# A causal decoder trunk on one core: the activation and weight buffers placed at chosen remainders of a KB

## The chip, the cores and the metric

The kernel runs on one core of one Trainium2 chip. The core has a matrix engine (TensorE, PE in the profile; PEld is its weight load), a vector engine (VectorE, DVE), a scalar engine (ScalarE, ACT), GpSimd (POOL) and a queue that issues DMAs (SyncE, SP). On-chip memory (SBUF) has 128 partitions, and a tile takes the same bytes in each of them; matmuls write to a separate memory, PSUM. The metric is the device time of one execution in microseconds, as a median of several.

## The reference

A trunk of two layers over 256 positions with 2048 features, in float32. Each layer: a norm, an attention mixer and a residual; a norm, a gated MLP with a causal convolution of width 3 and a residual; then a gated per-layer input and a residual.

```python
for i in range(DEPTH):                       # DEPTH = 2
    a = rmsnorm(h, attn_norm[i])
    h = h + (sb_dilated_mixer if i % 2 == 0 else fox_mixer)(a, ...)
    h = h + conv_ffn(rmsnorm(h, ffn_norm[i]), w_up[i], conv_w[i], conv_b[i], w_down[i])
    gate = jax.nn.sigmoid(rmsnorm(h, ple_norm[i]) @ w_ple_gate[i])
    h = h + gate * (p[i] @ w_ple[i])
return rmsnorm(h, final_norm)
```

Layer 0 mixes with 8 stick-breaking and 8 dilated heads, layer 1 with 16 heads that have forget gates. The feed-forward width is 5632. Nearly all the arithmetic is in the products with the weights: w_in, w_out, w_up, w_down and w_ple_gate, some 450 MB that are read once.

## The kernel before

Features lie on partitions and positions along the free axis. A float32 product is made of three products in a rounded format (float32r): each operand is split into a rounded part and the rest, and `PARTS` lists the three pairs that are summed (rest times rest is left out). An activation buffer `act0` or `act1` has the shape [128, 16, 2, 256]: 16 k tiles, and for each the rounded part and the rest, 256 positions of 4 bytes, so each such row is 1 KB. `pact` is a small one of the same kind for the per-layer input.

The weights come as a stream of *units* in the order of their use (`UNITS`). A unit is mostly 4 k tiles by 256 columns. `issue_group` brings one or two of them with one DMA of up to 1 MB into one of three raw buffers `wr` (L149). `split_unit` makes the two parts of a unit in a weight buffer `w`: ACT casts the rounded part (L165), DVE subtracts it from the raw value (L166). Of `w` there are four buffers of 8 KB, taken in rotation from a pool, each with rows of 1 KB (256 columns of a part of a k tile). `unit` keeps three split units ahead of the one in use.

`gemm_unit` (L203) runs the 24 matmuls of a unit: for each half j of the columns, each k tile and each of the three pairs, one matmul with 128 columns of `w` as the stationary operand and one row of `act` (256 positions) as the moving one. `gemm_v` (L237) has the roles the other way: a 128-position half row of `act` is stationary, 256 columns of `w` move. One block of layer 1, `gemm_vf` (L250), has 272 columns, since the forget gates' 16 columns are joined to the values', and its rows in `w` are 1088 bytes long.

The order of the work is written out by hand. Per pair of heads come q, k and v (psq, psk, psv); the attention's small float32 matmuls (scs, sps, avp) are deferred by some units (`defer`, `tick`) and so fall between the units of the next products. Then come w_out (pso), per group of 256 feed-forward features w_up (psu) twice, per block of 7 or 8 groups w_down (psd), and w_ple_gate (psg, in the last step pse). In layer 0, q, k, v, up and gate read act0, and out and down read act1; in layer 1 the two are swapped. The small per-layer product (psp) reads pact.

SBUF is handed out pool by pool, in the order in which the pools are opened, and within a pool in the order of the tiles: `cpool` with h (16 KB), act0, act1 (32 KB each), pact (4 KB), pl (16 KB) and small constants, then `wpool` with the three `wr` and four `w`, then `work` with the scratch tiles. `t2_tile` gives out scratch tiles of 2 KB from seven (for the feed-forward's yg and yv, the norm's squares and rows, the gates).

Of the kernel before, what the change touches and what calls it, by code (L numbers as in the profile page):

```python
# [10 lines left out]
F32 = mybir.dt.float32  # L11
F32R = mybir.dt.float32r
# [5 lines left out]
P = 128  # L18
D = 2048
S = 256  # L20
# [5 lines left out]
KT = D // P  # L26
# [78 lines left out]
def trunk(ctx: ExitStack, tc: tile.TileContext, xT, pT, pos, gains, conv, bf, cst, wst, out):  # L105
    nc = tc.nc

    cpool = ctx.enter_context(tc.tile_pool(name="cpool", bufs=1))
    wpool = ctx.enter_context(tc.tile_pool(name="wpool", bufs=1))
    work = ctx.enter_context(tc.tile_pool(name="work", bufs=1))  # L110
    psum = ctx.enter_context(tc.tile_pool(name="psum", bufs=1, space=bass.MemoryType.PSUM))

    h = cpool.tile([P, KT, S], F32, name="h")
    bufs = [cpool.tile([P, KT, 2, S], F32R, name=f"act{i}") for i in range(2)]
    pact = cpool.tile([P, 2, 2, S], F32R, name="pact")
    pl = cpool.tile([P, KT, S], F32, name="pl")
    gn = cpool.tile([P, 7, KT], F32, name="gn")
    cv = cpool.tile([P, DEPTH, 2 * FT, 4], F32, name="cv")
# [13 lines left out]
        return psum.tile([P, 2, 512], F32, name=name, tag="at", bufs=2)  # L132

    def t2_tile(name, shape=(P, 2, S), dt=F32):
        return work.tile(list(shape), dt, name=name, tag="t2", bufs=7)

    def t3_tile(name, shape=(P, 768), dt=F32):
        return work.tile(list(shape), dt, name=name, tag="t3", bufs=4)
# [3 lines left out]
    at = {"group": 0, "off": 0, "unit": 0, "tick": 0, "rows": 0}  # L142

    def issue_group():
        g = GROUPS[at["group"]]
        n = sum(u[3] * u[5] for u in g)
        raw = wpool.tile([P, 2048], F32, name="wr", tag="wr", bufs=3)
        src = wst[at["off"]:at["off"] + P * n].rearrange("(p f) -> p f", p=P)
        nc.sync.dma_start(out=raw[:, :n], in_=src)  # L149
        at["off"] += P * n  # L150
        at["group"] += 1
        o = 0
        for u in g:
            m = u[3] * u[5]
            raws.append((u, raw[:, o:o + m].rearrange("p (k c) -> p k c", c=u[5])))
            o += m

    def split_unit():
        if not raws:
            issue_group()  # L160
        u, raw = raws.pop(0)
        kc, cw = u[3], u[5]
        w = wpool.tile([P, 2048], F32R, name="w", tag="w", bufs=4)
        w = w[:, :2 * kc * cw].rearrange("p (k s c) -> p k s c", s=2, c=cw)
        nc.scalar.copy(out=w[:, :, 0, :], in_=raw)  # L165
        nc.vector.tensor_sub(out=w[:, :, 1, :], in0=raw, in1=w[:, :, 0, :].bitcast(F32))  # L166
        at["unit"] += 1
        ready.append((u, w))
# [3 lines left out]
    def unit(kind, l, k0, c0):  # L172
        while len(ready) < LOOK and at["unit"] < len(UNITS):
            split_unit()
        u, w = ready.pop(0)
        assert (u[0], u[1], u[2], u[4]) == (kind, l, k0, c0), (u, kind, l, k0, c0)
        return u[3], w
# [97 lines left out]
    def norm_squares(op):  # L275
        hs = h[:, 2 * op:2 * op + 2, :]
        if op == 0:
            nc.scalar.activation(out=acc, in_=hs, func=AF.Square)
        else:
            sq = t2_tile("sq")  # L280
            nc.scalar.activation(out=sq, in_=hs, func=AF.Square)
            nc.vector.tensor_add(out=acc, in0=acc, in1=sq)
# [26 lines left out]
    def norm_rows(mixer):  # L309

        dg = t2_tile("nd", (P, 2, P))
        ps = at_tile("rps")
        for t in range(2):
            nc.vector.tensor_scalar_mul(out=dg[:, t, :], in0=ident, scalar1=rT[:, t:t + 1])
            if mixer is None:
                nc.tensor.matmul(ps[:, 0, t * P:(t + 1) * P], lhsT=ones, rhs=dg[:, t, :],
                                 start=t == 0, stop=True, skip_group_check=True)
        if mixer is None:
            return ps[:, 0, :S]
        dh, dl = t2_tile("ndh", (P, 2, P), F32R), t2_tile("ndl", (P, 2, P), F32R)  # L320
        nc.scalar.copy(out=dh, in_=dg)
        nc.vector.tensor_sub(out=dl, in0=dg, in1=dh.bitcast(F32))
        for i, x in enumerate((dh, dl)):
            nc.tensor.matmul(ps[:, 0, :S], lhsT=trir[:, 0, :], rhs=x, start=i == 0, stop=i == 1)
        nc.vector.tensor_copy(out=rb, in_=ps[:, 0, :S])
        if mixer:
            nc.vector.tensor_scalar_mul(out=rq, in0=rb, scalar1=SCALE)
# [309 lines left out]
    for l in range(DEPTH):  # L637
        st = {}
        if l == 0:
            split_unit()  # L640
            rest_of_start()
            for op in range(8):
                ple_up(0, op)
            for i in range(8):
                norm_parts(i, 0, X)
            constants()

            def squares():
                for i in range(8):
                    norm_squares(i)  # L650

            defer(2, squares)
            norm_finish(True)
# [164 lines left out]
```

## Time and profile before

| | |
|---|---|
| Median of 3 runs | 2437.55 us (2437.21 to 2438.25) |
| The profiled execution | 2438.14 us |
| Its span, first to last instruction | 2436.3 us |
| Granted TensorE clock | 0.997 |
| Instructions | 48002 |
| HBM read | 452.86 MB, 187 GB/s over the span |

The profile is that of one execution. A line of the groups has the source line, the engine, the operation, what it writes and reads, how often, then the busy time and the mean of one in ns, then the idle time of the engine before it with what ended it. TensorE's matmuls overlap, so the mean of one (276 ns) is longer than the distance from one to the next. That distance is read from the chain in order of time, where a piece has its start, its length (both in us) and the number of its instructions.

### The profile page before, as it was taken

How to read it: one execution, taken by the hardware profiler on the slowest of the kernel's cores; microseconds unless marked ns; L12 is line 12 of the kernel's file. 1: busy time of each engine (PE TensorE's matmuls, PEld its weight loads, DVE VectorE, ACT ScalarE, POOL GpSimd, SP SyncE). 2: the span in 40 equal slices, each digit the busy share in tenths (PEclk: the TensorE clock that was granted, in tenths of full speed). 3: DMA queues.
4: the chain of work that ended last, by engine and by line, in shares of the span. 5: the costliest groups of instructions: out<-in, count | busy, mean ns of one | idle time of the engine just before them, and what ended most of it. 6: DMA issues, size and time to landing. Idle time of an engine off the chain costs nothing.

```text
span 2436.3 us, 48002 instructions
## 1 busy us (share of the span) xinstructions
PE 2414.1 (99%) x20990; PEld 2400.5 (99%) x20990; DVE 1595.7 (65%) x2157; ACT 1228.3 (50%) x1548; POOL 2.5 (0%) x8
## 2 busy tenths in 40 slices
PE   8999999999999999999999999999999999999997
PEld 8999999999999999999999999999999999999997
DVE  7557666776567657767765555677765776567676
ACT  6554455555355445555554444555543554455553
POOL 0000000000000000000000000000000000000000
PEclk9999999999999999999999999999999999999998
DMA  7444445555555555555554444555555555555553
GB/s 268 169 177 173 169 177 191 194 197 198 190 191 192 188 208 190 191 185 203 187 184 170 165 169 165 190 191 192 195 198 194 191 192 189 203 195 186 189 198 120
DMA packets 66483, 458.06 MB, mean 188 GB/s; under 512 B 7408, under 2 KB 7424, under 8 KB 16608
## 3 DMA queue, kind: packets, MB, share of 16 engines
q1 hardware_dynamic: 66096, 454.53, 52.8%
q8 instruction: 164, 2.69, 0.4%
q0 software_dynamic: 176, 0.46, 0.1%
q14 instruction: 47, 0.39, 0.0%
HBM read 452.86 MB, written 2.10 MB: 187 GB/s over the span
## 4 chain that ended last, share of the span: by engine, by line
PE 97%; DVE 1%; DMA 1%; ACT 1%; issue 0%; SPq 0%; DVEq 0%; ACTq 0%
PE psu L203 39%; PE psd L203 20%; PE pso L203 7%; PE psk L203 7%; PE psv L237 7%; PE psq L203 7%; PE psg L203 7%; DMA wr<-in_w 1%; PE avp L520 1%; PE psp L203 0%; PE pse L716 0%; PE scs L469 0%; PE psv L250 0%; PE sps L511 0%; PE avp L522 0%; PE scs L467 0%
## 5 line engine op out<-in xcount | busy, mean ns | idle before, releaser
L166 DVE TENSOR_TENSOR w<-wr,w 128x1024 fp32r<-128x1024 f32 (+2 forms) x882 | 1051.4, 1193 | 701.2 <-ACT w L165 695.5
L165 ACT CAST w<-wr 128x1024 fp32r<-128x1024 f32 (+2 forms) x882 | 905.6, 1028 | 1082.5 <-PE psu L203 355.1
L203 PE MATMUL psu<-act,w 128*128 128x256 f32 x8448 | 959.3, 276 | 0.0
L203 PEld LDWEIGHTS psu<-act,w 128*128 128x128 f32 x8448 | 958.3, 188 | 0.0
L203 PE MATMUL psd<-act,w 128*128 128x256 f32 x4224 | 479.7, 276 | 0.0
L203 PEld LDWEIGHTS psd<-act,w 128*128 128x128 f32 x4224 | 479.2, 188 | 0.0
L203 PE MATMUL psq<-act,w 128*128 128x256 f32 x1536 | 185.2, 279 | 1.2 <-DVE w L166 1.0
L203 PEld LDWEIGHTS psq<-act,w 128*128 128x128 f32 x1536 | 179.8, 188 | 2.1 <-DVE w L166 1.5
L203 PE MATMUL psk<-act,w 128*128 128x256 f32 x1536 | 180.0, 277 | 0.0
L203 PEld LDWEIGHTS psk<-act,w 128*128 128x128 f32 x1536 | 176.7, 188 | 0.0
L203 PE MATMUL pso<-act,w 128*128 128x256 f32 x1536 | 175.8, 277 | 0.0
L203 PEld LDWEIGHTS pso<-act,w 128*128 128x128 f32 x1536 | 174.9, 188 | 0.0
L237 PE MATMUL psv<-w,act 128*128 128x256 f32 x1440 | 172.7, 279 | 0.0
L237 PEld LDWEIGHTS psv<-w,act 128*128 128x128 f32 x1440 | 168.4, 188 | 1.1
L203 PE MATMUL psg<-act,w 128*128 128x256 f32 x1440 | 164.4, 276 | 0.0
L203 PEld LDWEIGHTS psg<-act,w 128*128 128x128 f32 x1440 | 163.7, 188 | 0.0
L616 DVE TENSOR_TENSOR u<-psu,rb 128x512 f32<-128x512 f32 x88 | 60.8, 691 | 33.3 <-PE psu L203 33.2
L622 DVE SCALAR_TENSOR_TENSOR yg<-u,cv,yg 128x256 f32<-128x256 f32 x176 | 73.3, 477 | 0.0
L622 DVE SCALAR_TENSOR_TENSOR yv<-u,cv,yv 128x256 f32<-128x256 f32 x176 | 73.3, 477 | 0.0
L619 ACT ACTIVATE yg<-u,cv 128x256 f32<-128x256 f32 x88 | 48.0, 594 | 1.0 <-DVE u L616 1.0
L619 ACT ACTIVATE yv<-u,cv 128x256 f32<-128x256 f32 x88 | 48.0, 593 | 0.0
L261 ACT CAST act<-yg 128x512 fp32r<-128x512 f32 x44 | 27.3, 621 | 39.1 <-DVE yg L632 39.1
(173 smaller groups left out, 886.5 us busy)
## 6 DMA issues: line engine op xcount, KB each, us to landing
wr<-in_w SPq DMA_DIRECT2D x388, 1024.0 KB, 4.8
wr<-in_w SPq DMA_DIRECT2D x36, 768.0 KB, 4.3
wr<-in_w SPq DMA_DIRECT2D x8, 896.0 KB, 4.6
wr<-in_w SPq DMA_DIRECT2D x7, 512.0 KB, 6.9
h<-in_x SPq DMA_DIRECT2D x4, 512.0 KB, 7.1
out_dram<-h SPq DMA_DIRECT2D x8, 256.0 KB, 2.4
wr<-in_w SPq DMA_DIRECT2D x2, 816.0 KB, 4.6
ct<-in_c SPq DMA_DIRECT2D x1, 841.0 KB, 6.6
```

The costliest lines, as they stand in the source:

```text
L165: nc.scalar.copy(out=w[:, :, 0, :], in_=raw)
L166: nc.vector.tensor_sub(out=w[:, :, 1, :], in0=raw, in1=w[:, :, 0, :].bitcast(F32))
L203: nc.tensor.matmul(ps[:, j, :], lhsT=w[:, k, s, js], rhs=act[:, k0 - koff + k, t, :], start=first and j + k + n == 0, stop=last and k == k ...
L237: nc.tensor.matmul(ps[:, t], lhsT=act[:, 4 * i + k, a, tsl], rhs=w[:, k, b], start=i + t + k + n == 0, stop=i == 3 and k == kc - 1 and n = ...
L261: nc.scalar.copy(out=dst[:, :, 0, :], in_=src)
L520: nc.tensor.matmul(av[:, 0, j * S:(j + 1) * S], lhsT=v[:, 0, js], rhs=w[:, j * S:(j + 1) * S], start=j == 0, stop=False, skip_group_check= ...
L616: nc.vector.tensor_mul(out=u[:, :, 2:], in0=ps, in1=rb2)
L619: nc.scalar.activation(out=y[:, j, :], in_=u[:, j, 2:], func=AF.Identity, bias=cv[:, l, t, 3:4], scale=cv[:, l, t, 2:3])
L622: nc.vector.scalar_tensor_tensor(out=y[:, j, :], in0=u[:, j, tap:tap + S], scalar=cv[:, l, t, tap:tap + 1], in1=y[:, j, :], op0=ALU.mult, ...
```

## The change

The activation and weight buffers move to the front of SBUF, into a pool of their own (`apool`). A helper `place` counts the bytes given out, from 16512 on, and puts an unused tile (gap) ahead of a buffer so that it starts at a chosen remainder of 1024: act0 at 0, act1 at 96, pact at 96, and the four weight buffers at 160, 256, 416 and 544. The weight buffers are four tiles with names, taken by the unit's number modulo 4, in place of four buffers of the pool `wpool`, which keeps the raw buffers and is opened ahead of `cpool`. The gaps take 1440 bytes. `t2_tile` has six tiles in place of seven. No instruction is added or removed.

```diff
+    apool = ctx.enter_context(tc.tile_pool(name="apool", bufs=1))
+    wpool = ctx.enter_context(tc.tile_pool(name="wpool", bufs=1))
     cpool = ctx.enter_context(tc.tile_pool(name="cpool", bufs=1))
-    wpool = ctx.enter_context(tc.tile_pool(name="wpool", bufs=1))
...
+    at_byte = [16512]
+
+    def place(shape, dt, name, rest):
+        n = (rest - at_byte[0]) % 1024
+        if n:
+            apool.tile([P, n // 4], F32, name=f"gap{at_byte[0]}")
+        t = apool.tile(shape, dt, name=name)
+        at_byte[0] += n + 4 * int(np.prod(shape[1:]))
+        return t
+
+    bufs = [place([P, KT, 2, S], F32R, f"act{i}", (0, 96)[i]) for i in range(2)]
+    pact = place([P, 2, 2, S], F32R, "pact", 96)
+    wbufs = [place([P, 2048], F32R, f"w{i}", (160, 256, 416, 544)[i]) for i in range(4)]
     h = cpool.tile([P, KT, S], F32, name="h")
-    bufs = [cpool.tile([P, KT, 2, S], F32R, name=f"act{i}") for i in range(2)]
-    pact = cpool.tile([P, 2, 2, S], F32R, name="pact")
...
-        return work.tile(list(shape), dt, name=name, tag="t2", bufs=7)
+        return work.tile(list(shape), dt, name=name, tag="t2", bufs=6)
...
-        w = wpool.tile([P, 2048], F32R, name="w", tag="w", bufs=4)
+        w = wbufs[at["unit"] % 4]
```

## The prediction

> **What bounds the kernel now.** I read the page first: the busy line, then the chain that ended last.
>
> ```profile
> PE 2414.1 (99%) x20990; PEld 2400.5 (99%) x20990; DVE 1595.7 (65%) x2157; ACT 1228.3 (50%) x1548; POOL 2.5 (0%) x8
> ...
> PE 97%; DVE 1%; DMA 1%; ACT 1%; issue 0%; SPq 0%; DVEq 0%; ACTq 0%
> PE psu L203 39%; PE psd L203 20%; PE pso L203 7%; PE psk L203 7%; PE psv L237 7%; PE psq L203 7%; PE psg L203 7%; DMA wr<-in_w 1%; PE avp L520 1%; PE psp L203 0%; PE pse L716 0%; PE scs L469 0%; PE psv L250 0%; PE sps L511 0%; PE avp L522 0%; PE scs L467 0%
> ```
>
> TensorE is never out of work: 97% of the chain is matmuls, and DVE (65%) and ACT (50%) have room. Who waits for whom says the same. ACT sits idle until matmuls free a weight buffer, while the longest wait of TensorE is 6.1 us in all, at the start.
>
> ```profile
> ACT w L165 <- PE psu L203: 355.1, 268, 2.1
> ...
> PE psp L203 <- ACT w L165: 6.1, 3, 5.6
> ```
>
> So the time is the number of matmuls times the distance from one start to the next, which I call the cadence. The chain in order of time gives it: a piece with its start, its length and its count. (In the groups of the page, busy over count says nearly the same: 959.3 us over 8448 is 113.6 ns.)
>
> ```profile
> 667.75 152.32 PE psu L203 x1344
> ...
> 2104.23 152.32 PE psu L203 x1344
> ```
>
> Both stretches, the first on act0 in layer 0 and the second on act1 in layer 1, have 152.32/1344 = 113.33 ns. The same lines show a second cadence.
>
> ```profile
> 231.28 8.16 PE psv L237 x72
> 239.44 0.22 PE scs L467 x2
> 239.66 0.43 PE scs L469 x2
> ...
> 240.75 2.83 PE psv L237 x24
> 243.58 8.48 PE psq L203 x72
> 252.06 0.65 PE sps L511 x6
> ```
>
> The matmuls of psv run at 8.16/72 = 113.33 ns, then a few fp32 matmuls of the attention come between, and the next ones run at 2.83/24 = 117.9 and 8.48/72 = 117.78 ns, on the same buffers, until the next interruption. So the cadence has two resting values, 113.33 and 117.78, and which one holds depends on when a run of matmuls starts. The third observation is the odd block of layer 1, 272 columns wide.
>
> ```profile
> 1212.64 6.73 PE psv L250 x54
> ```
>
> 6.73/54 = 124.6 ns. By its columns it should take 113.33 x 272/256 = 120.4 ns. What sets it apart is that its weight rows are 1088 bytes long, so the moving operand starts at another remainder of a KB, 64 bytes on, from one k tile to the next. This is the only stretch of the trace in which the remainder varies, and it is 4.2 ns per matmul slower than its width explains. I take from it that where an operand starts within a KB may matter to the cadence.
>
> **What the change does to that.** The remainders follow from the code. The new counter starts at byte 16512, which is 128 past a KB. Before, h lies there (16 KB), then act0, act1 and pact, all whole KBs: remainder 128 for all. The small constants behind them, each rounded up to 32 bytes, add 19,520 bytes (64 past a KB), so all seven weight buffers of 8 KB start at remainder 192. After, act0 is at 0, act1 and pact at 96, the weight buffers at 160, 256, 416 and 544.
>
> A matmul reads one operand from act and one from w. In the trace, the weight operand starts 64 or 576 bytes past the activations' remainder (L203, two column halves), or with the roles swapped (L237) 64 less or 448 more. All four distances are 64 more than a multiple of 128, and all have the cadence of 113.33 ns. After, the distances are 160, 256, 416, 544 with act0, and 64, 160, 320, 448 with act1. Those with act1 and the first, third and fourth weight buffers are again 64 more than a multiple of 128. The other five of eight are not. Each layer uses one activation buffer for q, k, v, up and gate and the other for out and down, and the layers swap them, so each of the eight pairs has about an eighth of the matmuls.
>
> The count: 8448 (psu) + 4224 (psd) + three times 1536 (psq, psk, pso) + 1440 (psv) + 1440 (psg) + 192 (psp) + 96 (pse) = 20,448 matmuls of 256 columns.
>
> ```profile
> L203 PE MATMUL psu<-act,w 128*128 128x256 f32 x8448 | 959.3, 276 | 0.0
> ...
> L203 PE MATMUL psd<-act,w 128*128 128x256 f32 x4224 | 479.7, 276 | 0.0
> ```
>
> Term 1, the cadence of the five eighths, 12,780 matmuls. No row shows a distance of the new kind in a matmul like these, so I bound it from both sides. The low end is the shortest cadence that the trace has with full weight loads: psq's neighbour above, sps L511, takes 0.65 us for 6, 108.3 ns (fp32, 128 columns). That would be 5.0 ns less each: -64 us. The high end is the second resting value, 117.78: 4.45 ns more each, +57 us. Between them I take 111.1 ns, about the middle between 108.3 and what it is now, because of the row that is nearest in kind:
>
> ```profile
> L203 PE MATMUL psu<-act,w x8448: 276/276/367, 405.6 to 2256.3; 128*128 128x256 f32 x197
> ```
>
> The shortest of psu's matmuls is as long as the median (276 ns): not one of them has shown a faster case, and the row at 108.3 streams fewer columns, so I don't count on the whole gap. 12,780 x (113.33 - 111.1) = 28.5 us off.
>
> Term 2, the slow stretches. In layer 0 each of eight heads' pairs has 72 matmuls of psq (pso at the last) and 24 or 48 of psv at 117.78; in layer 1 seven times 48 of psv; some 90 more at the start: about 1,250 in all.
>
> ```profile
> 1284.68 5.85 PE psv L237 x48
> ```
>
> Here 48 take 5.85 us, against 5.44 at 113.33 and 5.65 at 117.78 (the rest is the passage from the attention's operands). At 4.45 ns each they cost 5.6 us. If five eighths of them settle elsewhere, 3.5 us go; at worst more stretches turn slow, which is inside term 1's high end.
>
> Term 3, the 96 matmuls of 272 columns: from 120.4 to 128 ns, within 0.5 us either way. The fp32 matmuls of the attention also get other addresses. L469 above takes 0.43 us for 2 pieces, some 300 such pieces in all, and a difference of 4 ns in each would be 1.2 us. I take nothing for both.
>
> Term 4, the rotation of w by name in place of a pool's. The order of the four is the same, unit by unit. If the wait for a free buffer became one unit stricter, ACT would be the one that waits, and behind it DVE's subtraction.
>
> ```profile
> 700.49 1.05 ACT L165 CAST w<-wr 128x1024 fp32r<-128x1024 f32 x1 [1.68 <-PE psu L203]
> ...
> 701.57 1.23 DVE L166 TENSOR_TENSOR w<-wr,w 128x1024 fp32r<-128x1024 f32 x1 [0.45 <-ACT w L165]
> ```
>
> This unit is ready at 702.80, 2.3 us after its buffer came free, and it is used when three more units of 24 x 113.33 ns = 2.72 us have gone by, at about 708.6. One unit more is covered by these 5.8 us. Without the cover it would be 2.3 us per unit.
>
> Term 5, six t2 tiles in place of seven. A group of the feed-forward takes two of them.
>
> ```profile
> L619 ACT ACTIVATE yg<-u,cv x88: 586/594/604, 421.4 to 2247.2; 128x256 f32<-128x256 f32 x88
> ...
> L262 DVE TENSOR_TENSOR act<-yg,act x44: 683/683/687, 434.2 to 2262.3; 128x512 fp32r<-128x512 f32 x44
> ```
>
> The first group holds its tiles from 421.4 to 434.9, 13.5 us, and a new group starts every 152.32/7 = 21.8 us, so two groups at most overlap: four tiles. The three of the norm's row come with the first group alone. Cost nothing; DVE's third of idle time is the cover.
>
> Sum: 2438.1 (the profiled execution: its span of 2436.3 and 1.8 around it) - 28.5 - 3.5 = 2406; against the median of 2437.55, which lies 0.6 us lower, 2405.
>
> Faster matmuls would not run into another bound: at 111 ns a unit of 24 takes 2.66 us, DVE goes from 65% to 67%, and the weights' stream from 194 GB/s to 198, where the first slice shows 268.
>
> ```profile
> GB/s 268 169 177 173 169 177 191 194 197 198 190 191 192 188 208 190 191 185 203 187 184 170 165 169 165 190 191 192 195 198 194 191 192 189 203 195 186 189 198 120
> ```
>
> [...]
>
> **The rivals.**
> *The matmuls get slower.* The new distances rest at 117.78, as the stretches after an interruption do now. For it: that value is already there, and in the 272-column block, the only place with varying remainders, the excess over the width is 4.2 ns, nearly the same 4.45. Its place is every unit of one of the five changed pairs, its price +57 us with all five, giving 2494, and +28 with half of them. It decides as soon as the new pairs' resting cadence is above 113.33. Against it: the interruption alone, with unchanged addresses, puts the matmuls there, so it need not belong to any distance.
>
> *Only the slow stretches change.* If 113.33 is what a stream of 256 columns costs at best, and the remainders only decide in which of the two values a run settles, at most 5.6 us go: 2432. For it: the shortest psu is the median one.
>
> *Placement does nothing.* Then the cadence stays and the time is 2437.5 within 2. For it: ACT, DVE and the DMA come and go beside the matmuls without moving the 113.33. Against it: the 272-column row. [...]
>
> **How the numbers follow.** Faster through a shorter cadence, 2340 to 2430: 0.46, forecast 2405. Only the slow stretches, 2431 to 2436: 0.12, two thirds of which are past the 0.2% (5 us) that a measurement can tell from no change. Nothing: 0.09. Slower, 2443 to 2528: 0.33. So faster 0.54, within 0.2% 0.13, slower 0.33. The range: the low end with five eighths at 108.3 and no slow stretches is 2437.5 - 64 - 5.6 = 2368, and with all pairs at 108.3, 2330; the high end with five eighths at 117.78 is 2494, with all, 2528. I take 2350 to 2494, which leaves out some 0.15. The forecast's own range is 2350 to 2430.
>
> **What would show it.** In the chain in order of time, the long pieces of psu, psd, pso and psg: if their length over count differs between layers and buffers, placement acts. Term 1 is right if pieces of psu on act0 show less than 113.33 and some units of act1 stay there; wrong if all stay at 113.33 or go towards 117.78. Term 2 shows in the pieces of 72 behind the attention. Terms 4 and 5 are right if TensorE's waits stay at a few us and ACT's idle time before L165 is again for matmuls. The prediction fails if the cadence depends on something other than these distances, such as the weight buffers' places among themselves, or if the five changed pairs pull in both directions.

## The result and the profile after

| | before | after |
|---|---|---|
| Median | 2437.68 us (2437.21 to 2438.25, 4 runs) | 2511.04 us (2510.83 to 2511.19, 4 runs) |
| Span of the profiled execution | 2436.3 us | 2509.4 us |
| Granted TensorE clock | 0.997 | 0.997 |

The ratio is 1.0301, with a 95% interval of 1.0283 to 1.0319: 73 us slower. The clock is the same, so it is not a matter of throttling. The page of the changed kernel has the same shape as before: the busy line and the chain that ended last.

```profile
PE 2487.8 (99%) x20990; PEld 2475.0 (99%) x20990; DVE 1596.8 (64%) x2157; ACT 1226.8 (49%) x1548; POOL 2.5 (0%) x8
...
PE 98%; DVE 1%; ACT 0%; DMA 0%; issue 0%; SPq 0%; DVEq 0%
PE psu L216 39%; PE psd L216 20%; PE psk L216 7%; PE pso L216 7%; PE psq L216 7%; PE psv L250 7%; PE psg L216 7%; PE avp L533 1%; PE psp L216 0%; PE pse L729 0%; PE scs L482 0%; DMA wr<-in_w 0%; PE psv L263 0%; PE sps L524 0%; PE avp L535 0%; PE scs L480 0%
```

DVE has 1597 us of work as before, ACT 1227, and the count of matmuls is the same; TensorE alone is 73.7 us longer in use. The waits of the changed kernel (engine, line, for whom: us in all, times, longest) say that it waits for hardly anything; the largest item is 6.9 us in all, at the start:

```profile
ACT w L178 <- PE psu L216: 388.0, 268, 2.4
...
PE psp L216 <- ACT w L178: 6.9, 2, 5.4
```

So the matmuls themselves stand further apart. The chain in order of time (start, length, count) shows where. First psd of layer 0 in the kernel before, which runs at 76.16/672 = 113.33 ns:

```profile
820.07 76.16 PE psd L203 x672
```

Then the changed kernel, psu and psd of layer 0 and the same of layer 1:

```profile
686.35 160.52 PE psu L216 x1344
846.87 77.40 PE psd L216 x672
...
1934.74 154.56 PE psu L216 x1344
...
2089.30 80.19 PE psd L216 x672
```

Before, both psu stretches had 113.33 ns per matmul. Now psu on act0 has 160.52/1344 = 119.43 and psu on act1 154.56/1344 = 115.00; psd, which reads the other buffer, has 77.40/672 = 115.18 on act1 and 80.19/672 = 119.33 on act0. The cadence follows the activation buffer, not the line.

It also follows the weight buffer. A window that lies inside one unit cuts the chain to that unit's matmuls. Here are eight such answers of the changed kernel: four units that follow one another on act0 (weight buffers 1, 2, 3 and 0), then four on act1 (buffers 0, 1, 2 and 3).

```profile
700.56 2.75 PE psu L216 x23
703.44 2.87 PE psu L216 x24
706.31 2.72 PE psu L216 x23
709.27 2.64 PE psu L216 x22
...
1940.07 2.72 PE psu L216 x24
1942.91 2.64 PE psu L216 x22
1945.78 2.49 PE psu L216 x22
1948.39 2.61 PE psu L216 x23
```

Length over count is rounded here to some 0.4 ns: 119.6, 119.6, 118.3, 120.0 and 113.3, 120.0, 113.2, 113.5. The mean from the first start of a unit to the first start of the next, over the units of psu and psd, is sharper, and it is what the table has (65 to 68 units for each pair; those that other matmuls interrupt are left out). It is worked out from the start times in the trace, which no view prints unit by unit. The distance is the weight buffer's place less the activations', as in the prediction.

| | w0 | w1 | w2 | w3 |
|---|---|---|---|---|
| act0: distance | 160 | 256 | 416 | 544 |
| act0: ns per matmul | 119.56 | 119.81 | 119.68 | 118.58 |
| act1: distance | 64 | 160 | 320 | 448 |
| act1: ns per matmul | 113.75 | 119.58 | 113.40 | 113.40 |

Three pairs stand where all stood before; they are the three whose distance is 64 more than a multiple of 128. The other five lost 5.3 to 6.5 ns. Each pair has an eighth of 20,448 matmuls, 2556; the sum of the eight differences from 113.33 is 31.1 ns, so 79.5 us. From that go the slow stretches of before, which are now part of the rest (5.6 us): 73.9 us, against 73.4 measured. The pairs are measured in psu and psd alone. For these two the same sum gives 49.3 us, and the groups of the two pages have 49.4 (992.2 + 496.2 us busy against 959.3 + 479.7); that the rest comes out to half a us is partly luck.

### The profile page after: what moved, and what is told of

It reads as the page before. It is cut to its first block, busy times and chain, and to the rows that moved or that the text cites. A ratio compares the mean times of both kernels' runs of the same rounds, so it can differ in the third digit from the quotient of the medians.

```text
span 2509.4 us, 48220 instructions
## 1 busy us (share of the span) xinstructions
PE 2487.8 (99%) x20990; PEld 2475.0 (99%) x20990; DVE 1596.8 (64%) x2157; ACT 1226.8 (49%) x1548; POOL 2.5 (0%) x8
## 4 chain that ended last, share of the span: by engine, by line
PE 98%; DVE 1%; ACT 0%; DMA 0%; issue 0%; SPq 0%; DVEq 0%
PE psu L216 39%; PE psd L216 20%; PE psk L216 7%; PE pso L216 7%; PE psq L216 7%; PE psv L250 7%; PE psg L216 7%; PE avp L533 1%; PE psp L216 0%; PE pse L729 0%; PE scs L482 0%; DMA wr<-in_w 0%; PE psv L263 0%; PE sps L524 0%; PE avp L535 0%; PE scs L480 0%
## 5 line engine op out<-in xcount | busy, mean ns | idle before, releaser
L216 PE MATMUL psu<-act,w 128*128 128x256 f32 x8448 | 992.2, 280 | 0.0
L216 PEld LDWEIGHTS psu<-act,w 128*128 128x128 f32 x8448 | 991.1, 189 | 0.0
L216 PE MATMUL psd<-act,w 128*128 128x256 f32 x4224 | 496.2, 280 | 0.0
L216 PEld LDWEIGHTS psd<-act,w 128*128 128x128 f32 x4224 | 495.7, 188 | 0.0
L216 PE MATMUL psk<-act,w 128*128 128x256 f32 x1536 | 185.6, 280 | 0.0
L216 PEld LDWEIGHTS psk<-act,w 128*128 128x128 f32 x1536 | 182.3, 189 | 0.0
L216 PE MATMUL pso<-act,w 128*128 128x256 f32 x1536 | 181.4, 280 | 0.0
L216 PEld LDWEIGHTS pso<-act,w 128*128 128x128 f32 x1536 | 180.5, 189 | 0.0
L216 PE MATMUL psg<-act,w 128*128 128x256 f32 x1440 | 170.3, 280 | 0.0
L216 PEld LDWEIGHTS psg<-act,w 128*128 128x128 f32 x1440 | 169.6, 189 | 0.0
```

Source lines behind the costliest of these rows:

```text
L216: nc.tensor.matmul(ps[:, j, :], lhsT=w[:, k, s, js], rhs=act[:, k0 - koff + k, t, :], start=first and j + k + n == 0, stop=last and k == k ...
```

## The experiments

All kernels below come from the changed one. Each keeps its named weight buffers. The times are to be read beside 2437.4 to 2437.6 us, the medians of the kernel before that ran on the same chips. Two of the kernels were executed ten times, the others once. The first one below shows that executions of one kernel can lie 27 us apart, so where there is only one, the cadence in its trace says more than its time.

**Is it the places at all?** Two kernels put all distances back to 64 more than a multiple of 128, one with equal weight buffers and one with four different ones.

```diff
-    bufs = [place([P, KT, 2, S], F32R, f"act{i}", (0, 96)[i]) for i in range(2)]
-    pact = place([P, 2, 2, S], F32R, "pact", 96)
-    wbufs = [place([P, 2048], F32R, f"w{i}", (160, 256, 416, 544)[i]) for i in range(4)]
+    act 128, 128; pact 128; w 192, 192, 192, 192      (uniform)
+    act 128, 128; pact 128; w 192, 320, 448, 576      (four places)
```

> The changed kernel (weight buffers as named tiles, six scratch tiles, own pool first) with the remainders of the kernel before: act0, act1 and pact at 128, the four weight buffers all at 192, so every distance is 64. Theory distance (the cadence of a matmul follows from the distance between its two operands' places, modulo 128): every unit is back at 113.33 ns and the time is 2437 us within 3. Theory rotation (the named tiles, the six scratch tiles or the pools' order cost it): it stays near 2511.

> act0, act1 and pact at 128, the four weight buffers at four different remainders, 192, 320, 448 and 576, so that the distances are 64, 192, 320 and 448: all 64 more than a multiple of 128. Theory distance: 113.33 ns in every unit and 2437 to 2442 us, though no two weight buffers share a remainder. Theory among themselves (weight buffers at different remainders disturb each other, or each unit's first matmuls lose their lock): at least three quarters of the units slower, 2490 us or more.

The four places gave 2443.72 us in one execution, and in its long stretches the old cadence, 152.32/1344 = 113.33 ns; its chain in order of time:

```profile
668.49 152.32 PE psu L218 x1344
```

So unequal weight buffers do no harm to each other. Of the 6 us that are left, 4.5 are in psq and psv, whose runs lie between the attention's matmuls (187.8 and 174.6 us busy in the groups, against 185.2 and 172.7 before).

The uniform kernel has 113.33 ns too, but its ten executions fall on two values: five from 2435.25 to 2441.58 us, and five from 2463.34 to 2466.30. The granted clock is 0.997 to 0.998 in all ten, so throttling is not what parts them. The median of 2452.46 (ratio 1.0063, interval 1.0022 to 1.0104) is a mean of the two. The theory of distance had forecast 2437 within 3, which half of the executions miss. But both values are far from 2511, so neither the named buffers, nor six scratch tiles, nor the order of the pools is what costs. What the second value may be shows in the profiled execution, which took 2439.18 us. Its chain in order of time has psu of layer 0 and psg of layer 0:

```profile
665.08 152.32 PE psu L218 x1344
...
1136.40 76.32 PE psg L218 x648
```

psg, 648 matmuls without an interruption, ran at 76.32/648 = 117.78 ns from end to end. The same stretch of the kernel before:

```profile
1139.18 73.46 PE psg L203 x648
```

That is 113.36 ns. So the second resting value, which the prediction found behind the attention, can hold a long stretch too; what decides that it does is not shown. The feed-forward of one layer has 6216 matmuls in the rows from psu's 1416 to the last psd; at 4.45 ns each a whole one at the second value would be 27.6 us, the difference of the two groups of times. No trace shows such an execution, so this stays an inference.

**One part of the change undone.** First the activations, then the weights.

```diff
-    act 0, 96; pact 96; w 160, 256, 416, 544
+    act 96, 96; pact 96; w 160, 256, 416, 544         (activations undone)
+    act 0, 96; pact 96; w 160, 160, 160, 160          (weights undone)
```

> One part of the change undone: act0 is at 96 like act1 and pact, the weight buffers stay at 160, 256, 416 and 544. Distances 64, 160, 320 and 448 with both. Theory distance with the values measured in the changed kernel (64, 320 and 448: 113.33 ns; 160: 119.58): one quarter of 20448 matmuls 6.25 ns slower, 2437 + 32 = 2469 us. Theory that the weight buffers' unequal places do the harm: near 2511.

> The other part undone: act0 at 0 and act1 and pact at 96 as in the change, the weight buffers all at 160. Distance 160 with act0, 64 with act1. Theory distance: units on act0 119.58 ns, units on act1 113.33, half of the matmuls 6.25 ns slower, 2437 + 64 = 2501 us. Theory that the weight buffers' unequal places do the harm: near 2437.

They took 2472.65 and 2497.72 us, within 4 us of the sums of the theory of distance, and far from the other theory. The chains in order of time, psu of layer 0 and of layer 1, first with the activations undone:

```profile
907.02 154.56 PE psu L218 x1344
...
1902.51 154.56 PE psu L218 x1344
```

Both layers now have 115.00 ns, the value that act1 alone had. With the weights undone:

```profile
922.26 161.26 PE psu L218 x1344
...
1926.43 152.34 PE psu L218 x1344
```

act0 at distance 160 has 119.99 ns, act1 at distance 64 has 113.35. The harm lies in the pair. Undoing either part alone leaves those units slow whose distance is still off: half of them with equal weight buffers, a quarter with equal activation buffers.

**Is only the difference of the places what counts?** All buffers moved by 32 bytes, and all on places 16 past a multiple of 32. For the second, a tile is taken 32 bytes longer and used from byte 16 on.

```diff
+    act 160, 160; pact 160; w 224, 224, 224, 224      (shift by 32)
+    act 144, 272; pact 400; w 464, 592, 720, 848      (shift by 16)
```

> All buffers moved by 32 bytes against the uniform kernel: activations at 160, weight buffers at 224, every distance 64. Theory distance: only the difference counts, 113.33 ns, and the executions fall on the same two values as the uniform kernel's, about 2436 to 2442 and 2463 to 2466 us. If the place itself counts (blocks of 64 bytes): 118 ns or more, 2535 us.

> Places that are 16 more than a multiple of 32 for all (act0 144, act1 272, pact 400, weight buffers 464, 592, 720, 848), every distance 64 more than a multiple of 128. Theory distance: 113.33 ns, 2436 to 2442 or 2463 to 2466 us. If the place itself counts: 117 ns or more, 2510 us or more.

The shift by 32 gave 2436.11 us (2435.20 to 2436.98, ten executions; ratio 0.9994, interval 0.9984 to 1.0003): no difference from the kernel before that can be told, and none of its ten executions had the second value that half of the uniform kernel's had, though the same two values had been forecast. The chain has the old cadence:

```profile
665.30 152.32 PE psu L218 x1344
```

The shift by 16 gave 2449.68 us, which neither theory had forecast, and its chain shows a small loss:

```profile
669.53 153.07 PE psu L218 x1344
```

113.89 ns, 0.56 more than at 113.33, and each of the eight pairs lost about as much (113.8 to 114.0). So the difference is what counts to a first order, and places 16 bytes off the multiples of 32 cost a tenth of what a wrong distance does.

**Is there a distance that is better than 64?** Other multiples of 32, and distances a few bytes from 64.

```diff
+    act 128, 224; pact 128; w 224, 352, 512, 608      (multiples of 32)
+    act 128, 192; pact 192; w 196, 328, 464, 616      (a few bytes off)
```

> act0 and pact at 128, act1 at 224, the weight buffers at 224, 352, 512 and 608: distances 96, 224, 384, 480 with act0 and 0, 128, 288, 384 with act1. None is 64 more than a multiple of 128. Theory distance: every unit is slow, 118.5 to 120 ns as the five slow pairs of the changed kernel, so 2437 + 20448 x (118.6 to 119.9 - 113.33) = 2545 to 2572 us. Theory no rule (each distance has a value of its own): some unit is at or below 113.33 ns.

> Distances that are not multiples of 32: act0 at 128 with the weight buffers at 196, 328, 464 and 616 (64 + 4, 8, 16 and 40 past a multiple of 128), act1 and pact at 192 (4, 8, 16 and 40 past a multiple of 128). If the cadence goes by blocks of 64 or 32 bytes, the pairs with 4, 8 and 16 more than 64 stay at 113.33 and those with 4, 8 and 16 more than 0 are slow like 256 (119.9). If it goes by single elements, the cadence changes step by step between them, and a distance with less than 113.33 may lie between. About 2475 us in the first case.

With multiples of 32 the time was 2528.66 us. All eight new distances are slower than 113.33 ns, but less evenly than expected, and so the time is below the range given: by the mean over the units 117.8 (96), 116.6 (224), 118.9 (384) and 117.0 (480) on act0, 119.9 (0), 118.3 (128), 118.2 (288) and 118.7 (384) on act1. Some of these differ at the same distance modulo 128 (224 and 480 against 96; 0 against 128), so among the distances up to here only those 64 past a multiple of 128 have the good value (113.3 to 114.0 ns, against 116.6 to 120.0 at the others), but the size of the loss has no rule here. The chain, psu of layer 0 and of layer 1:

```profile
925.02 158.07 PE psu L218 x1344
...
1941.96 159.61 PE psu L218 x1344
```

A few bytes off 64 are as bad as 64 off: 2535.45 us, and already at 4 bytes (68) a unit on act0 has 118.25 ns, at 8 bytes 117.0, at 16 bytes 118.6. In its chain psu of layer 0 has 158.67/1344 = 118.06 ns.

```profile
690.22 158.67 PE psu L218 x1344
```

So the good distance is a point among those tried (4, 8, 16, 32 and 40 bytes past it and 32 short of it), not a range. In this last kernel the weight buffers also start 4, 8 or 16 bytes past a multiple of 32; places off by 4 or 8 bytes at a distance of 64 were not run, and off by 16 they cost 0.56 ns. None of the distances tried is better than 64.

**Can the cadence go below 113.33?** 113.33 ns is 17 steps of 6.67 ns, and the slow units on act0 with equal weight buffers have 120.0, which is 18 steps. I formed a theory that matmuls start on a grid of that step whose phase depends on the operands' places, and I tried to use it. (What gave me the idea is a reading of the raw start times of the kernel before, which no view here shows.) Rows of each k tile are made 64 bytes longer in act and w, and the 12 matmuls of a half unit (the same three products, in another order) go through the k tiles so that both operands move on by a fixed amount. The scratch tiles are five, and the shorter down blocks have k cuts of 4, 4, 4 and 2.

```diff
-            for k in range(kc):
-                for n, (s, t) in enumerate(PARTS):
+            todo = [(k, s, t) for s, t in ORDER for k in range(kc)]
+            for n, (k, s, t) in enumerate(todo):
...
+    todo for 128 bytes: k tiles 0, 2 in turn, then 1, 3;  64 back: range(kc - 1, -1, -1)
```

> Each k tile's row block is 64 bytes longer in act and w (so k tile k starts 64k past the first, modulo 256), distances of a matmul's own operands 64 as before, and the 12 matmuls of a half unit go through the k tiles 0, 2 in turn and then 1, 3, so that from one matmul to the next both operands move by 128 bytes. Theory grid: 113.33 ns is 17 steps of 6.67 ns, and matmuls start on a grid of that step whose phase moves with the operands' place, by about 1.67 ns for 64 bytes; 128 bytes from one to the next then give 113.33 - 3.33 = 110.0 ns (or 116.7, if a start cannot come earlier), 2369 us. Theory distance alone: 113.33 ns and about 2440 us.

> Same row blocks, k tiles in rising order for each of the three pairs, so 64 bytes from one matmul to the next; a matmul's own operands have distance 0, but its moving operand and the next matmul's weights have 64. Theory grid with the distance that counts taken to the next weights (which load while this matmul streams): 113.33 - 5.0 = 108.3 ns or 113.33 + 1.67 = 115.0 ns, 2335 or 2470 us. If the distance of a matmul's own operands counts: 119 to 120 ns as for distance 0 and 256 before, 2555 us or more.

> As the one before, with a matmul's own operands at distance 64 and 128 to the next weights. If the own distance counts: 108.3 or 115.0 ns, 2335 or 2470 us; if the distance to the next weights counts: 118 to 120 ns, 2540 us or more.

> As step64_base0 with the k tiles in falling order: 64 bytes back from one matmul to the next, distance 64 less (which is 64 more modulo 128) to the next weights. Theory grid with the next weights: 113.33 - 1.67 = 111.7 ns, 2403 us. With the own distance: 118 to 120 ns.

They took 2501.83, 2530.73, 2557.69 and 2531.69 us. The long stretches of psu in layer 0, one row from each chain, first with 128 bytes:

```profile
916.51 156.80 PE psu L225 x1344
```

64 bytes on, distance 0 (own operands):

```profile
926.97 159.04 PE psu L225 x1344
```

64 bytes on, distance 64:

```profile
935.47 161.27 PE psu L225 x1344
```

64 bytes back, distance 0:

```profile
927.22 159.04 PE psu L225 x1344
```

Per matmul these are 116.67, 118.33, 119.99 and 118.33 ns: 17.5, 17.75, 18 and 17.75 steps of 6.67. The first met the slower of the two values that the grid allowed it (116.7), and the theory of distance alone, which asked for 113.33, missed. The second, at 118.33, fits none of its forecasts. The third came out as forecast if the distance to the next weights counts (118 to 120 ns, 2540 us or more), the fourth as forecast if the own distance counts (118 to 120 ns). But by the first of these two rules the fourth had to be fast, and by the second the third. So neither distance is enough by itself. In the first kernel both are 64 more than a multiple of 128 in ten of twelve matmuls, and it was slow all the same.

What follows is narrower than what I set out for. Where the places move from one matmul to the next, a distance of 64 does not secure 113.33 ns; what else counts stays open. The order of the matmuls changed along with the rows, and no kernel has the new order with rows of whole KBs, so the order may have a share. No stream was brought below 17 steps, and the theory of a grid whose phase can be used is not borne out as I put it.

## Why the prediction was wrong

**What bounds the kernel** was read rightly: the time is matmuls times cadence, and that is all that moved.

**The distances** were the right variable. The forecast that three of eight pairs stay at 113.33 and five leave it came out pair by pair (113.40, 113.40 and 113.75 against 118.6 to 119.8), and with it the shares of the matmuls. The kernels with every distance at 64 past a multiple of 128 and the two with one part undone bear it out. The modulus of 128 was a guess that came true: in the kernel before only distances of 64 and 448 modulo 512 occur. The pair at 320 (113.40 ns) and the kernel with four places, which has 192 and 320, confirm it.

**Term 1 is the step that failed.** I bounded the cadence of a new distance by 108.3 ns below and by 117.78 above and took 111.1. It is 119.4 in the mean of the five pairs, outside both ends: in place of 28.5 us off, 12,780 x (119.4 - 113.33) = 78 us on. Both the direction and the size of the term were wrong, and no row had shown a gain. The low end came from fp32 matmuls of 128 columns, another stream altogether, and no distance since tried brought these matmuls below 113.33. The row on psu's shortest matmul, which I quoted, could not decide it either way: all 8448 stood at the old good distances, so it could show neither the gain nor the loss of another.

The odd block of 272 columns was the only row of the weights' products at other distances, and its excess was a loss. But it is a weak sign. I read its rows as moving on by 64 bytes from one k tile to the next; it is 64 from a k tile's rounded part to its rest, and 128 from tile to tile, so that the rests alone, in one matmul of three, stand off the good distance. And no run has 272 columns at one remainder, so what of the 4.2 ns belongs to the width and what to the places is not shown.

**The high end** was too low for a like reason: 117.78 was the second resting value of the old distance, not a bound on other distances. The rival that the matmuls get slower was the right one, with the right place (the five pairs) and the point from which it decides; its price was +57 us, and it cost 79.5 less the 5.6 of the slow stretches. Why a wrong distance costs some 6 ns is not shown by any run.

**Term 2**: the stretches behind the attention were expected to gain 3.5 us. They are now at the general level of their pairs. In the changed kernel's chain, psq of layer 0:

```profile
59.91 8.61 PE psq L216 x72
```

That is 119.6 ns in place of 117.78.

**Term 3** was right: the 272-column block takes 6.79/54 = 125.7 ns in place of 124.6, 0.1 us in all.

```profile
1254.58 6.79 PE psv L263 x54
```

**Terms 4 and 5** were right: the shift by 32 keeps the named buffers and six scratch tiles, and is at 0.9994 of the kernel before. The uniform kernel's psg, 117.78 ns over 648 matmuls, shows that a stretch can settle at the second value in the changed arrangement, though the shift by 32 had no such time in ten executions.

**The rival that placement does nothing** fell. In the kernel with equal weight buffers psu took 119.99 ns on act0 at 0 and 113.35 on act1 at 96, beside the same work of the other engines. The changed kernel shows no wait for another engine that would account for the loss either: the largest item of TensorE's waits is 6.9 us in all, and the loss is 73. That it is a conflict inside the memory is not shown by any run.

## What to carry to other kernels

When matmuls are back to back with new weights each time, look at the cadence from start to start for each pair of buffers, not at the busy share, which was 99% before and after. In this kernel, with rows of whole KBs, a float32r matmul of 256 columns had its best cadence (113.3 to 114.0 ns, against 116.6 to 120.0) only where the two operands' places differed by 64 more than a multiple of 128 bytes. The kernel before had that by luck: between its activation and weight buffers lie tiles of whole KBs and 19,520 bytes of small constants, which is 64 past a KB. With whole KBs alone the distance would have been 0, which took 119.9 ns in the kernel with multiples of 32. So a tile of another size between the two can cost 3 to 4% (2511 to 2535 us here). And where a trace shows a value as a floor with no exception in thousands, a price below it needs a row of its own kind.

## What was not expected of the hardware

The cadence moved with places of operands that differ by 4 bytes (113.33 ns at a distance of 64, 118.25 at 68 in the kernel with a few bytes off), while ACT, DVE and the DMA beside it left no mark: in the kernel before, all four stretches of 1344 matmuls of psu took 152.32 us. In the kernel before, matmuls on the same buffers ran at two values, 113.33 ns (psv, 8.16/72) and, behind the attention's matmuls, 117.78 (psq, 8.48/72); the uniform kernel's psg held the second for 648 matmuls. And many of the values are quarter steps of 6.67 ns: 17 (113.33), 17.5 (116.67), 17.75 (118.33) and 18 (120.0); 117.78 is 17 2/3 steps and so is not one. What makes the step is not known from these runs.
